# A hybrid decoder step on one core: block loads moved ahead of head loads, casts freed from ScalarE's copies, and an input split moved later

## The chip, the cores and the metric

The kernel runs on one core of a Trainium2 chip. The metric is the device time of one launch in microseconds. Five engines run side by side, each working through its own row of instructions in order: TensorE (PE, with its weight loads listed as PEld), VectorE (DVE), ScalarE (ACT), GpSimd (POOL) and SyncE, whose queue (SPq) issues most of the transfers. They meet by semaphores.

## What is computed

One layer of a decoder over 1024 prompt rows and 32 sample rows (8 sequences of 4), width 1024. The input is normalised and modulated, multiplied by a wide input matrix, and goes through two branches: an mLSTM with matrix memory (4 heads, chunks of 128) and sliding-window attention (8 query heads, 2 key heads, window 128, a sink per head). Each branch is gated and projected, the two are mixed by sigmoid gates, projected once more and added to the input.

```python
h, gate = adaln_in(x, c, w_ada, b_ada, g_norm)
(mq, mk, mv, mi, mf, mo, mz, aq, ak, av, az, gm, ga) = split_in(h @ w_in)
y_m, C, n, m = mlstm_branch(mq, mk, mv, mi, mf, mo, mz, C0, n0, m0, b_i, b_f, g_mn)
...
y_a = o.astype(x.dtype) * jax.nn.silu(az)
u = jax.nn.sigmoid(gm) * (y_m @ w_mo) + jax.nn.sigmoid(ga) * (y_a @ w_ao)
x = x + gate * (u @ w_o)
```

## The kernel before

All matmuls of the big projections are done in three products of rounded halves: each operand is split into a hi part (a cast to the rounded format, mostly on ACT) and a lo part (the remainder, a subtraction on DVE or GpSimd), and hi x hi, lo x hi and hi x lo are summed in PSUM. So every weight tile and every input tile passes through a cast and a subtraction before PE can use it. The names say which is which: `wh_...` and `wl_...` are the halves of a weight, `ym_l` and `ym_h` are the buffers of the halves of the gated mLSTM output (the names are those of the quarter of memory that they lie in: `ym_l` holds the hi part, `ym_h` the lo part).

The program runs in stages. First come the modulation and the first column groups. Then the queries of attention (`g_aq`) and the first head's `mq`, `mk`, `mv` and the second head's `mq` (`g_mq`) are computed column group by column group with plain products. From there the remaining input columns are computed in pairs as 2 x 2 blocks with seven products instead of eight (`block_products`, L1639). The stage that follows, the attention branch's output projection, uses the same scheme in four groups (`att_products`, L1851), and its products are written to PSUM tiles `ax`, `aw`, `az` and `ay`. Then the mLSTM output projection (`g_w_mo`) and the last projection (`fo...`) follow.

The code is written as one stream that emits PE's instructions in their final order. Beside it run generators (`Side`, L113): attention units, head steps, loads, sample work. Each generator yields an estimated time; when the emitted PE work has advanced that far it is resumed and emits its next piece. The rows of ACT and DVE are then put in order by a scheduler, which places an instruction early if its inputs look ready. What is emitted may be tied down with order-only links: `no_sync` (L215) puts one instruction of an engine behind another without a semaphore, and the wrapper `Ordered` (L225) links every ACT instruction that is emitted to those in `S.floor`, if there are any. `emptied` (L588) sets that floor to the copy just emitted:

```python
        def emptied(ins):
            if not products_done or begun_att:
                S.floor = [getattr(ins, "ins", ins)]
```

In the attention output stage it is called on every copy from one PSUM tile to another (`aw` from `ax`, `ay` from `aw`) and on the copy `p5` of `az`, and the floor stands until the next one.

Three places matter here.

The first block loads: `sum_blocks` (L1424) forms sums of input blocks for the seven products. Its second half waits until `plain_ends` is set (L1114, at the last plain job), polls every 0.5 us of planned time, loads two pairs of blocks `hb` from DRAM (four transfers of 256 KB), yields 3.0, and subtracts in each pair on DVE. The loads of the first head's first chunks (`hq`, `hk`, `hv`, `et`, `qw`; `load`, L1136) come from another generator at about the same place. All these tiles come from one rotating pool of 50 buffers (`ht`, L207), so the place in the row decides which old buffer a load has to wait for. Two attention units are under way there: `unit` (L894) computes scores `sc`, masks them on DVE with a row maximum (the custom operations into `p` and `mx`), exponentiates on ACT and transposes (`pt`) into PSUM; a copy brings `pt` back into `p`. The sample attention (`sample_attention`, L1003) ends with two transposes into `ost`. The tiles `pt`, `smp` and `ost` share the two PSUM buffers of the pool `pb` (L201).

The output stage's casts: `split` of `AttPair` (L1832) casts a weight block on ACT and subtracts on DVE for the seven products of one group; `split_ahead` in `att_products` calls it two products ahead. The names carry the group and the home: `ao0B` is group 0, home B, which serves product 6 and then product 2; `ao0C` serves 7 and 3, `ao0D` 4, `ao1A` the next group's 1 and 5. At the same time the last input gates (`hg`, L1612) and the sums of the attention output (`att_sums`, L1745, tiles `yr`, `yat...`, `yab...`) are still being finished on ACT, DVE and GpSimd.

The next stage's input: the mLSTM output `ymD` is loaded from DRAM and split into `ym_l` and `ym_h` (`split`, L1368), one quarter at product 6 of groups 0, 1 and 3 and one at product 3 of group 2.

Of the kernel before, what the change touches and what calls it, by code (L numbers as in the profile page):

```python
# [186 lines left out]
def body(tc, a):  # L187
    nc = tc.nc
    with ExitStack() as ctx:
# [17 lines left out]
        def ht(shape, name, dt=F32):  # L207
            return sp.tile(shape, dt, tag="half", bufs=50, name=name)
# [50 lines left out]
        V, S, G = Ordered(nc.vector, "V"), Ordered(nc.scalar, "S"), Ordered(nc.gpsimd, "G")  # L259
# [311 lines left out]
        def piece(w, rh, rl, kn, name, p, evac):  # L571
# [13 lines left out]
            evac(p, acc, c0, n)  # L585
            side.tick()

        def emptied(ins):  # L588
            if not products_done or begun_att:
                S.floor = [getattr(ins, "ins", ins)]  # L590

        def clear():
            while side.left <= 4:
                yield 0.0, ""

        hs, begun_att = {}, []

        def h_hi(k, c0, n, x="h"):
            ks = k
# [765 lines left out]
                store(a["n_s"], at["n1"])  # L1365


        def split(src, his, los, cols, k, eng=V):  # L1368
            for i, c in enumerate(cols):
                raw = ht([128, 512], "yr")[:, :c.stop - c.start]  # L1370
                dma(raw, src[k][:, c])
                hi, lo = his(k, c.start, c.stop - c.start), los(k, c.start, c.stop - c.start)
                S.copy(hi, raw)
                eng.tensor_tensor(lo, raw, hi.bitcast(F32), op=ALU.subtract)
# [49 lines left out]
        def sum_blocks():  # L1424
            names = "t3", "t2", "t4"
            for n in names:
                blocks[n] = []
            for k in range(4):
                b11, b12, b21, b22 = (xT[th][4 * kh + k] for kh in range(2) for th in range(2))
                for n in names:  # L1430
                    block_tiles(n, k)
                V.tensor_tensor(b22, b22, b12, op=ALU.subtract)
                yield 2.5, ""
                V.tensor_tensor(b11, b11, b22, op=ALU.add)
                V.tensor_tensor(b21, b21, b11, op=ALU.subtract)
                yield 4.0, ""
                for n, t in zip(names, (b22, b11, b21)):
                    block_split(n, k, t)
                    yield 3.0, ""
            formed.append("t2")  # L1440
            while not plain_ends:
                yield 0.5, ""
            load = lambda k: block_load(((0, 0), (0, 1)), k)
            ts = [load(0), load(1)]
            yield 3.0, ""
            for b11, b12 in ts:
                V.tensor_tensor(b12, b12, b11, op=ALU.subtract)
            while not products_done:
                yield 0.5, ""
            for k in range(4):  # L1450
                b11, b12 = ts[k]
                if k > 1:
                    V.tensor_tensor(b12, b12, b11, op=ALU.subtract)
                block_split("t1", k, b12)
                if k < 2:
                    ts.append(load(k + 2))
                yield 1.5, ""
            formed.append("t1")
# [180 lines left out]
        def block_products(jobs, hook):  # L1639
# [27 lines left out]
            for j, (n, i) in enumerate(flat):  # L1667
# [31 lines left out]
                if i == 6:  # L1699
                    Y = filled(pa, "by", W, n)  # L1700
                elif i == 2:
                    job_.done(0, 0, X)
                    gated_ = [job_.weighted] if job_.kind is query_gate else []
                elif i == 5:
                    p5 = ht([128, 512], "p5")
                    emptied(S.copy(p5, Z))
                elif i == 3:
                    job_.done(0, 1, p5, W)
                elif i == 4:
                    job_.done(1, 0, Y)  # L1710
# [140 lines left out]
        def att_products():  # L1851
# [23 lines left out]
            jobs[0].split(5)  # L1875
            yield
            ut.extend(quarter(x, [128, 4, PITCH], "u") for x in ("h1", "l1"))
            begun_att.append(True)
            for j, (n, i) in enumerate(flat):
                job_ = jobs[n]  # L1880
                nxt = jobs[n + 1] if n < 3 else None
                if i == 6:
                    if nxt:
                        nxt.landed = [last["PE"]]
                        nxt.gates()
                    if n in (0, 1, 3):
                        split(ymD, *ymx, PCOLS, {0: 2, 1: 3, 3: 1}[n], G if n == 3 else V)
                if i == 3 and n == 2:
                    split(ymD, *ymx, PCOLS, 0)
                if i == 2 and not nxt:  # L1890
                    for d in range(4):
                        preload(("w_mo", d))
                split_ahead(j + 2)
                if i == 3 and not nxt:
                    prefetch(("w_mo", 0))
                    gated(("w_mo", 0))
                if i == 1:
                    o = NX = pg([128, 512], "ax")
                elif i == 5:
                    o = Z = pa([128, 512], "az")  # L1900
                else:
                    o = {2: lambda: X, 3: lambda: W, 4: lambda: Y, 6: lambda: W, 7: lambda: Y}[i]()
                new = i in (1, 5)
                wh, wl = job_.w.pop(i)
                for k in range(2):
                    side.until(lambda: k in ya[OPERANDS[i]])
                    bh, bl = ya[OPERANDS[i]][k]
                    mm(o, wh[:, k], bh, start=(new and k == 0), stop=False, more=not new)
                    mm(o, wh[:, k], bl, start=False, stop=False, more=not new)
                    mm(o, wl[:, k], bh, start=False, stop=(k == 1), more=not new)  # L1910
                    side.tick()

                def copy_of(pool, name, src):
                    t = pool([128, 512], name)
                    if n == 0 and (j == 0 or i == 6):
                        mm(t, job_.g["A"][0][:, 0], ya["b11"][0][0], start=True, stop=True)
                    emptied(S.copy(t, src))
                    return t

                if i == 6:  # L1920
                    Y = copy_of(pa, "ay", W)
                    if not nxt:
                        job_.samples_end()
                elif i == 2:
                    job_.done(0, 0, X)
                    if nxt:
                        job_.samples_end()
                        side.now += nxt.cost
                        nxt.first_sums()
                elif i == 5:  # L1930
                    p5 = ht([128, 512], "p5")
                    emptied(S.copy(p5, Z))
                elif i == 7:
                    job_.done(1, 1, p5, Y)
                elif i == 3:
                    job_.done(0, 1, p5, W)
                elif i == 4:
                    job_.done(1, 0, Y)
                if j == 0 or (i == 3 and nxt):
                    X = NX  # L1940
                    W = copy_of(pg, "aw", X)
            S.floor = []


        def run(gen):
# [602 lines left out]
```

## Time and profile before

| what | value |
|---|---|
| time of three runs | 818.04, 820.47, 820.71 us, median 820.47 |
| the profiled execution's own time | 818.98 us |
| its span | 817.2 us |
| granted TensorE clock, mean | 0.996 |
| PE busy | 799.9 us, 98% of the span |
| DVE busy | 599.3 us, 73% |
| ACT busy | 419.0 us, 51% |
| POOL busy | 79.7 us, 10% |
| transfers | 165.51 MB, mean 203 GB/s |

The profile is of one execution. A row of a timeline gives the start in us from the span's start, the duration, the engine, the line, the operation and its tiles as out<-in, and in brackets how long the engine was idle before it and what ended that. Almost all computing instructions bear line 233 or 296, which are the helpers that record them; they are told apart by their tiles. PE matmuls overlap: the time that one costs is the distance from its start to the next start. A DMA instruction on SPq is only its issue; when the data lands is seen from who waits for it.

### The profile page before, as it was taken

The page shows a single profiled execution, that of the slowest core. Times are in us where ns is not written, and L with a number is a line of the kernel's source. Part 1 is how long each engine was busy: PE and PEld are TensorE (multiplying, and loading weights), DVE is VectorE, ACT ScalarE, POOL GpSimd, SP SyncE. Part 2 cuts the span into 40 slices and gives each one's busy share as a digit, 9 for nine tenths or more (in the row PEclk, how much of TensorE's full clock was granted, in tenths as well). Part 3 has the DMA queues.
Part 4 walks back from the last instruction along what each step waited for, and adds up shares of the span by engine and source line. Part 5 has one row for each costly group of instructions (what it writes and reads, how often), then busy time and mean ns, then how long its engine had stood idle before and what let it go on. Part 6 is the DMA issues. An engine that isn't in the chain of part 4 may idle for free. (4 is left out here: it accounts for less than half of the span.)

```text
span 817.2 us, 15181 instructions
## 1 busy us (share of the span) xinstructions
PE 799.9 (98%) x5162; PEld 669.0 (82%) x5162; DVE 599.3 (73%) x1502; ACT 419.0 (51%) x1021; POOL 79.7 (10%) x156
## 2 busy tenths in 40 slices
PE   8999999997999999999999999999999999999996
PEld 5779898896888888888888888888888779997775
DVE  5899986745756557476568888898668998875666
ACT  5664355654565564546656545554446553124335
POOL 0120000010000000000001323231002201000000
PEclk9999999999999999999999999999999999999999
DMA  9995667554744433547764685866246589748632
GB/s 351 375 340 159 209 191 194 180 174 143 213 154 142 140 102 134 155 150 239 253 217 132 248 255 193 285 208 195 101 135 209 171 279 347 262 150 294 207 104 110
DMA packets 113794, 165.51 MB, mean 203 GB/s; under 512 B 21248, under 2 KB 55936, under 8 KB 113684
## 3 DMA queue, kind: packets, MB, share of 16 engines
q1 hardware_dynamic: 107316, 152.21, 56.9%
q10 hardware_dynamic: 4752, 7.60, 2.5%
q0 software_dynamic: 1648, 4.72, 1.5%
q8 instruction: 41, 0.67, 0.3%
q14 instruction: 37, 0.30, 0.1%
HBM read 115.51 MB, written 50.00 MB: 203 GB/s over the span
## 5 line engine op out<-in xcount | busy, mean ns | idle before, releaser
L233 ACT ACTIVATE p<-p,nmx 128x256 f32<-128x256 f32 (+1 forms) x64 | 30.9, 484 | 17.6 <-DVE nmx L233 12.8
L233 DVE CUSTOM_DVE_ANT_0 p<-sc,cst,sink 128x256 f32<-128x256 f32 (+1 forms) x64 | 26.1, 463 | 13.2 <-PE sc L296 13.2
L233 POOL TENSOR_SCALAR Cs<-Cs,sxb 128x129 f32<-128x129 f32 x32 | 28.1, 896 | 42.4 <-PE sn L296 42.4
L296 PE MATMUL g_aq<-h_h,wh_aq 128*128 128x384 f32 (+1 forms) x96 | 32.2, 336 | 0.0
L296 PE MATMUL g_aq<-h_h,wl_aq 128*128 128x384 f32 (+1 forms) x96 | 30.9, 322 | 0.0
L296 PE MATMUL g_aq<-h_l,wh_aq 128*128 128x384 f32 (+1 forms) x96 | 30.8, 321 | 0.0
L296 PE MATMUL g_w_mo<-ym_l,wh_w_mo 128*128 128x384 f32 (+1 forms) x96 | 30.8, 321 | 0.0
L296 PE MATMUL g_w_mo<-ym_l,wl_w_mo 128*128 128x384 f32 (+1 forms) x96 | 30.8, 321 | 0.0
L296 PE MATMUL g_w_mo<-ym_h,wh_w_mo 128*128 128x384 f32 (+1 forms) x96 | 30.8, 321 | 0.0
L233 ACT CAST wosh<-wor 128x512 fp32r<-128x512 f32 x24 | 14.8, 621 | 14.0 <-DVE wor L233 13.2
L282 POOL DMA_DIRECT2D oD<-p x16 | 8.7, 544 | 132.5 <-ACT p L233 62.9
L233 DVE COPY p<-pt 128x512 f32<-128x512 f32 (+1 forms) x16 | 10.5, 657 | 14.8 <-PE pt L301 14.6
L296 PEld LDWEIGHTS g_aq<-h_h,wh_aq 128*128 128x128 f32 x96 | 18.0, 188 | 2.5 <-issue 1.5
L233 DVE TENSOR_TENSOR wosl<-wor,wosh 128x512 fp32r<-128x512 f32 x24 | 16.5, 686 | 3.3 <-ACT wosh L233 3.2
L233 DVE SCALAR_TENSOR_TENSOR tgw_mo<-tgw_mo,g_w_mo 128x384 f32<-128x384 f32 (+1 forms) x24 | 12.4, 518 | 8.1 <-PE g_w_mo L296 7.3
L296 PEld LDWEIGHTS g_w_mo<-ym_l,wl_w_mo 128*128 128x128 f32 x96 | 18.0, 188 | 0.1
L233 ACT ACTIVATE aq<-g_aq 128x384 f32<-128x384 f32 (+1 forms) x12 | 5.6, 463 | 24.4 <-PE g_aq L296 24.4
L296 PEld LDWEIGHTS g_w_mo<-ym_l,wh_w_mo 128*128 128x128 f32 x96 | 18.0, 188 | 0.0
L296 PEld LDWEIGHTS g_aq<-h_l,wh_aq 128*128 128x128 f32 x96 | 18.1, 188 | 0.0
L296 PEld LDWEIGHTS g_w_mo<-ym_h,wh_w_mo 128*128 128x128 f32 x96 | 18.0, 188 | 0.0
L296 PEld LDWEIGHTS g_aq<-h_h,wl_aq 128*128 128x128 f32 x96 | 18.0, 188 | 0.0
L233 DVE TENSOR_TENSOR et<-et,S 128x384 f32<-128x384 f32 (+1 forms) x12 | 6.1, 509 | 15.8 <-PE S L296 15.8
(2068 smaller groups left out, 2848.5 us busy)
## 6 DMA issues: line engine op xcount, KB each, us to landing
early_h<-w_ada SPq DMA_DIRECT2D x8, 512.0 KB, 10.1
adar_ga<-w_ada SPq DMA_DIRECT2D x16, 256.0 KB, 3.9
wr_ga<-w SPq DMA_DIRECT2D x16, 256.0 KB
wr_gm<-w SPq DMA_DIRECT2D x16, 256.0 KB, 6.8
taD<-gt SPq DMA_DIRECT2D x16, 256.0 KB, 2.3
tmD<-gt SPq DMA_DIRECT2D x16, 256.0 KB, 2.1
wor<-w_out SPq DMA_DIRECT2D x16, 256.0 KB, 7.3
tga<-taD SPq DMA_DIRECT2D x16, 256.0 KB, 3.5
```

The source lines that it names most:

```text
L233: ins = f(*args, **kw)
L282: ins = (eng or nc.sync).dma_start(out, in_)
L296: in_order(nc.tensor.matmul(out, lhsT, rhs, start=start, stop=stop, skip_group_check=more))
```

## The change

Three edits go together.

In `sum_blocks` the poll for `plain_ends` yields 0.0 instead of 0.5, so it is resumed at the next step of the planner, and the wait between loads and subtractions is 7.0 instead of 3.0 of planned time.

In `att_products` the floor is no longer set by `emptied` and no longer stands from copy to copy. The copies `aw` and `ay` are remembered in `emptied_last`, the copies `p5` are not, and the floor is set around `split_ahead` alone, from the third step on (j > 1), with the split of the next stage's input inside it.

The split of `ymD` is divided into its loads and its casts with subtractions. For groups 0 and 1 the loads stay at product 6, and the casts and subtractions move to product 4. For groups 2 and 3 nothing is divided.

```diff
         def emptied(ins):
-            if not products_done or begun_att:
-                S.floor = [getattr(ins, "ins", ins)]
+            if not products_done:
+                S.floor = [copy_made(ins)]
...
-        def split(src, his, los, cols, k, eng=V):
-            for i, c in enumerate(cols):
-                raw = ht([128, 512], "yr")[:, :c.stop - c.start]
+        def split_load(src, cols, k):
+            raws = [ht([128, 512], "yr")[:, :c.stop - c.start] for c in cols]
+            for raw, c in zip(raws, cols):
                 dma(raw, src[k][:, c])
+            return raws
+
+        def split(src, his, los, cols, k, eng=V, raws=None):
+            for c, raw in zip(cols, raws or split_load(src, cols, k)):
...
             while not plain_ends:
-                yield 0.5, ""
+                yield 0.0, ""
             load = lambda k: block_load(((0, 0), (0, 1)), k)
             ts = [load(0), load(1)]
-            yield 3.0, ""
+            yield 7.0, ""
...
-                    if n in (0, 1, 3):
-                        split(ymD, *ymx, PCOLS, {0: 2, 1: 3, 3: 1}[n], G if n == 3 else V)
+                    if n == 3:
+                        split(ymD, *ymx, PCOLS, 1, G)
+                    elif n < 2:
+                        ym_raws = split_load(ymD, PCOLS, n + 2)
...
+                if j > 1:
+                    S.floor = list(emptied_last)
                 split_ahead(j + 2)
+                if i == 4 and n < 2:
+                    split(ymD, *ymx, PCOLS, n + 2, V, ym_raws)
+                S.floor = []
...
-                    emptied(S.copy(t, src))
+                    emptied_last[:] = [copy_made(S.copy(t, src))]
...
                     p5 = ht([128, 512], "p5")
-                    emptied(S.copy(p5, Z))
+                    S.copy(p5, Z)
```

PE's row is the same in both kernels but for numbers in names. What moves is on SPq, DVE and ACT.

SPq's row at the end of the plain jobs, before; `hq` to `qw` are the first head's five loads, `hb_0` and `hb_1` the two pairs of blocks, the rows ahead and behind are a weight and the next attention unit's keys:

```order
L282 DMA wr_w_mo_0_2451<-w_mo 128x512
L282 DMA hq_0_2457<-qD_137 128x384
L282 DMA hk_0_2458<-kD_138 128x384
L282 DMA hv_0_2459<-vD_139 128x384
L282 DMA et<-nmd 128x384
L282 DMA qw<-wid 128x384
L282 DMA hb_0_2467<-hD 128x512
L282 DMA hb_0_2469<-hD 128x512
L282 DMA hb_1_2471<-hD 128x512
L282 DMA hb_1_2473<-hD 128x512
L282 DMA uqk<-kD 128x384
```

The same place of SPq's row now:

```order
L282 DMA wr_w_mo_0_2451<-w_mo 128x512
L282 DMA hb_0_2457<-hD 128x512
L282 DMA hb_0_2459<-hD 128x512
L282 DMA hb_1_2461<-hD 128x512
L282 DMA hb_1_2463<-hD 128x512
L282 DMA hq_0_2465<-qD_137 128x384
L282 DMA hk_0_2466<-kD_138 128x384
L282 DMA hv_0_2467<-vD_139 128x384
L282 DMA et<-nmd 128x384
L282 DMA qw<-wid 128x384
L282 DMA uqk<-kD 128x384
```

The four block loads stand ahead of the head's five, in the first four of the nine places, and nothing else has moved in this row in the whole program.

DVE's row at the same time, before; `ws` is a sum of weights, the ISA rows are the mask operations of one attention unit with their row maxima, and the COPY is that of another unit's transposed probabilities:

```order
L233 TENSOR_TENSOR ws_2591<-wr_mv_0_2447,wr_mv_1_2449 128x512
L233 TENSOR_TENSOR hb_0_2469<-hb_0_2469,hb_0_2467 128x512
L233 ISA p_2542,mx<-sc_4_0_2545,cst,sink 128x256
L233 ISA mx 128x1
L233 ISA p_2542,mx<-sc_4_0_2545,cst,sink 128x256
L233 ISA mx 128x1
L233 TENSOR_TENSOR hb_1_2473<-hb_1_2473,hb_1_2471 128x512
L233 ISA p_2543,mx<-sc_4_1_2546,cst,sink 128x256
L233 ISA mx 128x1
L233 ISA p_2543,mx<-sc_4_1_2546,cst,sink 128x256
L233 ISA mx 128x1
L233 COPY p_2301<-pt_0_1_2563 128x384
```

The same place of DVE's row now:

```order
L233 TENSOR_TENSOR ws_2589<-wr_mv_0_2447,wr_mv_1_2449 128x512
L233 TENSOR_TENSOR hb_0_2459<-hb_0_2459,hb_0_2457 128x512
L233 TENSOR_TENSOR hb_1_2463<-hb_1_2463,hb_1_2461 128x512
L233 ISA p_2540,mx<-sc_4_0_2543,cst,sink 128x256
L233 ISA mx 128x1
L233 ISA p_2540,mx<-sc_4_0_2543,cst,sink 128x256
L233 ISA mx 128x1
L233 ISA p_2541,mx<-sc_4_1_2544,cst,sink 128x256
L233 ISA mx 128x1
L233 ISA p_2541,mx<-sc_4_1_2544,cst,sink 128x256
L233 ISA mx 128x1
L233 COPY p_2301<-pt_0_1_2561 128x384
```

The second subtraction has moved ahead of the two mask operations that stood between the two; the copy is still behind both.

DVE's row in group 0 of the output stage, before; `hg` are the last input gates, `u_h` the gated results of the stage:

```order
L233 TENSOR_TENSOR yat2l_7779<-yr,yat2h_7778 128x512
L233 SCALAR_TENSOR_TENSOR hg_7688<-hg_7758,hg_7688 128x512
L233 TENSOR_TENSOR hg_7688<-hg_7688,ho 128x512
L233 SCALAR_TENSOR_TENSOR hg_7785<-hg_7785,by 128x512
L233 SCALAR_TENSOR_TENSOR hg_7785<-hg_7660,hg_7785 128x512
L233 TENSOR_TENSOR yr<-yr 128x512
L233 TENSOR_TENSOR hg_7785<-hg_7785,ho 128x512
L233 TENSOR_TENSOR wl_ao0B<-wr_ao_7592,wh_ao0B 128x256
...
L233 TENSOR_TENSOR yat4l_7855<-yr,yat4h_7854 128x512
L233 TENSOR_TENSOR ym_h_7557<-yr,ym_l_7556 128x384 x2
L233 TENSOR_TENSOR ym_h_7557<-yr,ym_l_7556 128x288
L233 SCALAR_TENSOR_TENSOR u_h_7790<-tga,u_h_7790 128x512
```

The same places of DVE's row now:

```order
L233 TENSOR_TENSOR yat2l_7779<-yr,yat2h_7778 128x512
L233 TENSOR_TENSOR wl_ao0B<-wr_ao_7592,wh_ao0B 128x256
L233 SCALAR_TENSOR_TENSOR hg_7688<-hg_7758,hg_7688 128x512
...
L233 TENSOR_TENSOR yat4l_7849<-yr,yat4h_7848 128x512
L233 SCALAR_TENSOR_TENSOR u_h_7790<-tga,u_h_7790 128x512
L233 TENSOR_TENSOR wl_ao0D<-wr_ao_7593,wh_ao0D 128x256
...
L233 TENSOR_TENSOR wl_ao1B<-wr_ao_7490,wh_ao1B 128x256
L233 TENSOR_TENSOR ym_h_7557<-yr,ym_l_7556 128x384 x2
L233 TENSOR_TENSOR ym_h_7557<-yr,ym_l_7556 128x288
L233 TENSOR_TENSOR wl_ao1B<-wr_ao_7490,wh_ao1B 128x256
```

The lo part for product 2 (`wl_ao0B`) has moved ahead of six instructions, and the three `ym_h` have moved from ahead of `wl_ao0D` to between the two `wl_ao1B` of the next group. On ACT the first cast into `wh_ao0B` has moved ahead of the cast of `yab22h`, and the second from behind the copy `aw` to the first one's old place.

More of the change, by code (lines that the diff above doesn't have):

```diff
@@ L586, in piece @@
             side.tick()
+        copy_made = lambda ins: getattr(ins, "ins", ins)
         def emptied(ins):
-            if not products_done or begun_att:
-                S.floor = [getattr(ins, "ins", ins)]
+            if not products_done:
+                S.floor = [copy_made(ins)]
         def clear():
@@ L594, in clear @@
                 yield 0.0, ""
-        hs, begun_att = {}, []
+        hs = {}
         def h_hi(k, c0, n, x="h"):
@@ L1877, in att_products @@
             ut.extend(quarter(x, [128, 4, PITCH], "u") for x in ("h1", "l1"))
-            begun_att.append(True)
+            emptied_last = []
             for j, (n, i) in enumerate(flat):
@@ L1931, in att_products @@
                     p5 = ht([128, 512], "p5")
-                    emptied(S.copy(p5, Z))
+                    S.copy(p5, Z)
                 elif i == 7:
@@ L1941, in att_products @@
                     W = copy_of(pg, "aw", X)
-            S.floor = []
         def run(gen):
```

## The prediction

> **What bounds the kernel now.** I read the page first, then the waits of TensorE (PE), then the timelines of PE, VectorE (DVE), ScalarE (ACT) and the load queue (SPq) around each of those waits, and last the chain of waits. The page's span and engine rows:
>
> ```profile
> span 817.2 us, 15181 instructions
> PE 799.9 (98%) x5162; PEld 669.0 (82%) x5162; DVE 599.3 (73%) x1502; ACT 419.0 (51%) x1021; POOL 79.7 (10%) x156
> ```
>
> PE is busy for 98% of the span, so all that a change of order can win is 817.2 - 799.9 = 17.3 us of idle PE, and whatever PE loses by running slowly. The waits of PE, longest first (total, times, longest), name three places of interest here:
>
> ```profile
> PE ost L301 <- DVE p L233: 4.1, 1, 4.1
> ...
> PE ay L296 <- DVE wl_ao0D L233: 0.9, 1, 0.9
> ...
> PE ax L296 <- DVE wl_ao0B L233: 0.8, 1, 0.8
> ```
>
> All three are waits for DVE. The first sits where the head loads and the first block loads are issued, the two others at the start of the output products of the attention branch: the two places that the change touches. After 652.61 us the chain of waits runs on PE alone to 787.7 us; its longest and its last piece before that:
>
> ```profile
> 681.78 45.96 PE g_w_mo L296 x288
> ...
> 784.96 2.73 PE foW L296 x12
> ```
>
> So what PE gains at either place arrives at the end, unless a later wait takes it back.
>
> **Part 1: the first blocks' loads.** PE's timeline (start, duration) around the first wait:
>
> ```profile
> 191.76 0.33 PE L296 MATMUL g_mq<-h_l,wh_mq 128*128 128x384 f32 x1
> 191.93 0.34 PE L296 MATMUL g_mq<-h_h,wl_mq 128*128 128x384 f32 x1
> 196.41 0.69 PE L301 MATMUL ost<-cst,ps 128*128 128x128 f32 x2 [4.14 <-DVE p L233]
> 196.75 0.67 PE L296 MATMUL g_mq<-h_h,wh_mq 128*128 128x384 f32 x1
> ...
> 199.78 0.36 PE L296 MATMUL g_mq<-h_h,wh_mq 128*128 128x384 f32 x1
> ```
>
> Matmuls of this shape start 0.17 us apart. The `ost` transposes would start at 191.93 + 0.17 = 192.10; they start at 196.41, so 4.3 us are lost. Then nine matmuls take 199.78 - 196.75 = 3.03 us where nine spacings are 9 x 0.17 = 1.53: another 1.5 us. The windows (busy us of PE, PEld, DVE, ACT and POOL, then the granted clock) show why:
>
> ```profile
> 196.00:198.00 2.00, 1.59 (x6) 1.59 (x7) 1.97 (x6) 1.49 (x6) 0.00 (x0) 0.60 0.52 199
> 198.00:200.00 2.00, 2.00 (x9) 2.00 (x8) 1.93 (x7) 1.19 (x5) 0.00 (x0) 0.55 0.00 0
> ```
>
> The granted clock is 0.60 and 0.55 right after the wait. The place costs 4.3 + 1.5 = 5.8 us. A rule for the second share: the Trainium skill, "TensorE: Matmul & The Clock Gate", section "Part 1: The HAM clock gate", has the clock halved after an idle window of about 3.4 us and restored after about 3.4 us of work, which as an estimate loses 1.7 us; by that page the place would cost 6.0 us. The trace agrees in kind (199.78 - 196.41 = 3.4 us at about half clock).
>
> Why PE waits: `ost` takes a PSUM buffer of the pool `pb`, of which there are two, and its last reader is DVE's copy of the transposed probabilities. DVE's timeline:
>
> ```profile
> 184.96 0.68 DVE L233 TENSOR_TENSOR ws<-wr_mv,wr_mv 128x512 f32<-128x512 f32 x1
> 191.01 0.69 DVE L233 TENSOR_TENSOR hb<-hb,hb 128x512 f32<-128x512 f32 x1 [5.37 <-DMA hb<-hD]
> 191.72 0.48 DVE L233 CUSTOM_DVE_ANT_0 p<-sc,cst,sink 128x256 f32<-128x256 f32 x1
> ...
> 194.38 0.69 DVE L233 TENSOR_TENSOR hb<-hb,hb 128x512 f32<-128x512 f32 x1 [1.77 <-DMA hb<-hD]
> ...
> 195.80 0.55 DVE L233 COPY p<-pt 128x384 f32<-128x384 f32 x1
> ```
>
> DVE is held twice, 5.37 and 1.77 us, by the two block subtractions, and the copy that PE needs is queued behind both. It ends at 196.35, and PE starts 0.06 us later. The loads, on SPq's timeline and in its waits between 176 and 187 us:
>
> ```profile
> 177.68 0.38 SPq L282 DMA_DIRECT2D hq<-qD  x1
> ...
> 184.65 0.32 SPq L282 DMA_DIRECT2D qw<-wid  x1
> 185.07 1.80 SPq L282 DMA_DIRECT2D hb<-hD  x4
> ```
>
> ```profile
> SPq L282 <- DMA vD<-mk: 13.6, 2, 8.5
> ```
>
> Four head loads go out from 177.68 on; the fifth, `qw`, is held until 184.65 by the landing of a `vD` store, and the four block loads stand behind it. The order shows the block loads in the first four places now, with the head's five behind them; the wait belongs to the place in the row (a buffer or a semaphore used before), so it will hold `hq`, the new fifth. The block loads then go out 7.4 us earlier (177.68 for 185.07). At worst they landed 194.38 - 185.07 = 9.3 us after the first was issued; from 177.68 that is 187.0. From there DVE needs at most one more subtraction (0.69), four mask operations (0.48 each, 1.9) and the copy (0.55): 187.0 + 3.2 = 190.2. PE asks at 192.1. The wait goes whole, with 1.9 us to spare, and the clock stays up: 5.8 us. Bounds: 6.0 above (the pair of transposes itself at full clock saves some 0.2 more), 5.1 below (a wait of 0.7 us, one DVE operation, for whatever is late next).
>
> What is late next is the head: its five loads now leave where the block loads left, from 184.65, and at the same worst landing arrive by 194.4. They are wanted here:
>
> ```profile
> 199.90 0.56 DVE L233 TENSOR_TENSOR et<-et,cst 128x384 f32<-128x384 f32 x1
> 203.57 0.49 PE L301 MATMUL tk<-cst,hk 128*128 128x128 f32 x3
> ```
>
> With everything 5.8 us earlier DVE asks for `et` at 194.1 and PE for `hk` at 197.8. DVE may wait 0.3 us, PE has 3.4 us to spare: nothing, as long as that cover stands; beyond it, 1 us per us.
>
> **Part 2: casts without a floor in the first two groups, and the split of the next stage's input later.** PE and then DVE:
>
> ```profile
> 644.06 0.39 PE L296 MATMUL ax<-yab21h,wh_ao0B 128*128 128x512 f32 x1
> 644.28 0.39 PE L296 MATMUL ax<-yab21l,wh_ao0B 128*128 128x512 f32 x1
> 645.48 0.50 PE L296 MATMUL ax<-yab21h,wl_ao0B 128*128 128x512 f32 x1 [0.81 <-DVE wl_ao0B L233]
> 645.82 0.39 PE L296 MATMUL ax<-yab21h,wh_ao0B 128*128 128x512 f32 x1
> ...
> 651.29 0.39 PE L296 MATMUL ay<-yat4l,wh_ao0D 128*128 128x512 f32 x1
> 652.61 0.50 PE L296 MATMUL ay<-yat4h,wl_ao0D 128*128 128x512 f32 x1 [0.93 <-DVE wl_ao0D L233]
> ```
>
> ```profile
> 645.02 0.41 DVE L233 TENSOR_TENSOR wl_ao0B<-wr_ao,wh_ao0B 128x256 fp32r<-128x256 f32 x1
> ...
> 650.23 1.38 DVE L233 TENSOR_TENSOR ym_h<-yr,ym_l 128x384 fp32r<-128x384 f32 x3
> 651.54 0.68 DVE L233 SCALAR_TENSOR_TENSOR u_h<-tga,u_h 128x512 f32<-128x512 f32 x1
> 652.14 0.41 DVE L233 TENSOR_TENSOR wl_ao0D<-wr_ao,wh_ao0D 128x256 fp32r<-128x256 f32 x1
> ```
>
> With a spacing of 0.23, the first wait costs 1.20 - 0.23 = 0.97 us and 0.11 for the slow restart (0.34 to the next start), the second 1.09 and as much again: 2.3 us, the ceiling. The first goes: `wl_ao0B` is now ahead of the six DVE instructions that stood between it and `yat2l`. For the second, DVE works without a pause up to `wl_ao0D`; its busy time is the third in this window's row:
>
> ```profile
> 639.40:652.50 13.10, 11.46 (x52) 8.82 (x50) 12.93 (x28) 7.24 (x17) 1.54 (x1) 1.00 0.63 194
> ```
>
> The set of instructions ahead of that one is the same as before but for the three `ym_h` subtractions, 651.54 - 650.23 = 1.3 us (the three loads keep their place in SPq's row). So `wl_ao0D` ends 1.3 us earlier and PE restarts at 651.3: PE comes to this wait 1.1 us earlier and finds most of it still there. The two waits together give 1.3, not 2.3.
>
> Against that stands a cast that now comes early in ACT's row: the hi part `wh_ao0B` before `yab22h`. It needs a weight buffer that PE still reads for its product 7:
>
> ```profile
> 631.72 0.39 PE L296 MATMUL by<-t3h,wl_phead_gate__7603 128*128 128x512 f32 x1
> 631.69 0.61 ACT L233 CAST yab22h<-yr 128x512 fp32r<-128x512 f32 x1
> ```
>
> The buffer is free at 632.11, the cast takes about 0.3 us, so `yab22h` starts at 632.4 or 632.5, 0.8 us late, and behind it the subtraction on GpSimd and the DVE instruction that waits for that. If nothing catches that up, 0.5 of the 1.3 is left. I take 1.2, because 20 us lie between that cast and `wl_ao0D`, and each wait of DVE for ACT or GpSimd in them takes up part of the delay; ends 0.5 and 2.3.
>
> Who pays for the later split: the same three `ym_h` now stand between the two `wl_ao1B`, which ended here:
>
> ```profile
> 654.73 0.75 DVE L233 TENSOR_TENSOR wl_ao1B<-wr_ao,wh_ao1B 128x256 fp32r<-128x256 f32 x2
> 656.86 0.39 PE L296 MATMUL ax<-yab21h,wl_ao1B 128*128 128x512 f32 x1
> ```
>
> Taken out ahead and put in again, they leave the end of the second `wl_ao1B` at 655.48, while PE asks 1.2 us earlier, at 655.66: 0.2 us of cover, and any miss costs its own length. The same move in the second group and the dropped floor behind the copy of `az` have no PE wait near them; I cost both at nothing.
>
> **Sum.** 5.8 + 1.2 = 7.0 us. The profiled execution took 818.98 us (span 817.2 and 1.8 around it): 812.0. It is 1.5 us below the median of the three timed runs, 820.47, from which the same sum gives 813.5. I forecast 813.0, between the two and nearer the median. A measurement of this kernel can tell about 0.3%, 2.5 us, from no change.
>
> **Rivals.**
> A wait that shrinks (10%): the block loads share their time with other transfers and land later than 187.0, by 4 us, say; then DVE's copy ends at 194.2 and PE still waits 2.1 us. Against it: the four places went out without a pause before. For the clock, the rows say that waits of 0.81 and 0.93 us are followed by a matmul of 0.50 and then by 0.39 again, so a wait of that size brings no slow clock; 4.14 does. The gain is 5.8 - 2.1 + 1.2 = 4.9, time 815.6.
>
> No gain in part 2 (16%): the early cast or the thin cover of 0.2 us eats the 1.2, or 0.5 more. Gain 5.3 to 5.8, time 814.7 to 815.2.
>
> Given back later (8%): PE's 7 us run into a load that does not move with PE in the last 160 us. Speaking against it, the chain of waits there is PE alone. Time 818 to 820.5.
>
> Slower (4%): the wait grows. All four mask operations and the copy now stand behind both subtractions, where two stood ahead of the second. If the second block landed only at 194.4, PE would start at 197.6, which is 1.2 later than now and eats part 2; from there on every us costs one. At a landing of 198 the time is 824.1. The point from which this decides is 16.7 us after the first issue, against 9.3 seen.
>
> **How the numbers follow.** The forecast has 62%, its own gain running from 5.1 + 0.5 to 6.0 + 2.3, that is 5.6 to 8.3 us: 809.7 (from the lowest run, 818.04) to 815.1 (from 820.71). With the first two rivals the range goes from 810.0 to 816.5. Faster by over 0.3%: 62 + 10 + 16 = 88%; within 0.3%: 8%; slower: 4%.
>
> **What will show it.** Right: no PE wait on `ost`; granted clock 1.00 in the windows that hold the nine `g_mq` matmuls; `hb` loads issued near 177.7 and DVE not idle ahead of the subtractions; `hq` held to about 184.7; `ax` without a wait on `wl_ao0B`, a wait of 0.6 to 1.0 us left on `wl_ao0D`; span near 810. Wrong: a PE wait on `ost`, `tk` or `tv` above 1 us, a PE wait on `wl_ao1B`, or `wl_ao0D` ending no earlier relative to PE's `ax`.

## The result and the profile after

The kernel after takes 811.95 us (median of 4 runs, 811.18 to 812.10) against 819.64 us of the kernel before (median of 4 runs beside it, 818.04 to 820.71): a ratio of 0.9906, 95% interval 0.9886 to 0.9926. The profiled execution took 812.10 us. From its page, the span and the engine row:

```profile
span 810.3 us, 15182 instructions
PE 798.5 (99%) x5162; PEld 668.2 (82%) x5162; DVE 598.8 (74%) x1502; ACT 418.5 (52%) x1021; POOL 78.9 (10%) x156
```

The span is 6.9 us shorter, PE's busy time 1.4 us: most of what went was idle PE, the rest is matmuls at the full clock. Where it went is read from four matmuls that PE runs in the same order in both kernels: the first `smp` (ahead of the first place), the first `tk` (behind it), the first `ax` and the first `g_w_mo` (ahead of and behind the groups of the output stage). PE's timeline of the kernel before (start, duration):

```profile
188.90 0.30 PE L296 MATMUL smp<-wr_mk,c 128*32 128x128 f32 x2 [0.24 <-ACT p L233]
...
203.57 0.49 PE L301 MATMUL tk<-cst,hk 128*128 128x128 f32 x3
...
639.50 0.39 PE L296 MATMUL ax<-ym_l,wh_ao0A 128*128 128x512 f32 x1
...
681.62 0.33 PE L296 MATMUL g_w_mo<-ym_l,wh_w_mo 128*128 128x384 f32 x1
```

and of the kernel after:

```profile
189.49 0.30 PE L296 MATMUL smp<-wr_mk,c 128*32 128x128 f32 x2 [0.24 <-ACT p L233]
...
198.25 0.49 PE L301 MATMUL tk<-cst,hk 128*128 128x128 f32 x3
...
634.19 0.39 PE L296 MATMUL ax<-ym_l,wh_ao0A 128*128 128x512 f32 x1
...
674.75 0.33 PE L296 MATMUL g_w_mo<-ym_l,wh_w_mo 128*128 128x384 f32 x1
```

| stretch of PE's row, us | before | after | difference |
|---|---|---|---|
| start to `smp` | 188.90 | 189.49 | +0.59 |
| `smp` to `tk` | 14.67 | 8.76 | -5.91 |
| `tk` to `ax` | 435.93 | 435.94 | 0.0 |
| `ax` to `g_w_mo` | 42.12 | 40.56 | -1.56 |
| `g_w_mo` to the end of the span | 135.58 | 135.55 | 0.0 |

Two stretches changed, at the two places of the change, and nothing was given back: from `tk` to `ax` PE took 435.9 us in both. The 0.59 us ahead of `smp` lies where the two programs are the same; a second profile of the kernel after had `smp` at 188.86. These two stretches are the measure in what follows, since they leave the scatter of the start out.

**The first place.** PE's row at `ost`, the windows (us of PE, PEld, DVE, ACT, POOL, then the granted clock) over the matmuls behind it, DVE, and the load queue, all of the kernel after:

```profile
192.52 0.34 PE L296 MATMUL g_mq<-h_h,wl_mq 128*128 128x384 f32 x1
192.69 0.38 PE L301 MATMUL ost<-cst,ps 128*128 128x128 f32 x2
192.83 0.42 PE L296 MATMUL g_mq<-h_h,wh_mq 128*128 128x384 f32 x1
```

```profile
192.00:194.00 2.00, 2.00 (x14) 1.97 (x14) 1.45 (x7) 1.75 (x7) 0.00 (x0) 1.00 0.93 235
194.00:196.00 2.00, 2.00 (x16) 1.97 (x15) 1.94 (x5) 0.80 (x2) 0.00 (x0) 1.00 0.56 159
```

```profile
185.54 0.69 DVE L233 TENSOR_TENSOR ws<-wr_mv,wr_mv 128x512 f32<-128x512 f32 x1
186.15 1.29 DVE L233 TENSOR_TENSOR hb<-hb,hb 128x512 f32<-128x512 f32 x2
188.57 0.48 DVE L233 CUSTOM_DVE_ANT_0 p<-sc,cst,sink 128x256 f32<-128x256 f32 x1 [1.14 <-issue]
...
190.19 0.55 DVE L233 COPY p<-pt 128x384 f32<-128x384 f32 x1
```

```profile
178.28 1.80 SPq L282 DMA_DIRECT2D hb<-hD  x4
186.49 0.32 SPq L282 DMA_DIRECT2D hq<-qD  x1
```

`ost` starts one spacing behind the matmul ahead of it. The two subtractions follow `ws` without a wait, the copy that frees `ost`'s PSUM buffer ends at 190.74, 1.95 us before PE asks, and the clock behind `ost` is 1.00 where it was 0.60 and 0.55. The hold of the queue is still there; it now stands ahead of `hq`.

**The second place.** PE's and DVE's rows:

```profile
641.71 0.40 PE L296 MATMUL ay<-yat3h,wl_ao0C 128*128 128x512 f32 x1
642.87 0.47 PE L296 MATMUL ax<-ym_l,wh_ao1A 128*128 128x512 f32 x1 [0.76 <-DVE u_h L233]
...
646.13 0.40 PE L296 MATMUL ay<-yat4h,wl_ao0D 128*128 128x512 f32 x1
```

```profile
635.28 0.42 DVE L233 TENSOR_TENSOR wl_ao0B<-wr_ao,wh_ao0B 128x256 fp32r<-128x256 f32 x1
...
638.43 0.69 DVE L233 TENSOR_TENSOR yr<-yr 128x512 f32<-128x512 f32 x1 [0.60 <-POOL yab21l L233]
...
642.04 0.68 DVE L233 SCALAR_TENSOR_TENSOR u_h<-tga,ax 128x512 f32<-128x512 f32 x1
...
645.51 0.42 DVE L233 TENSOR_TENSOR wl_ao0D<-wr_ao,wh_ao0D 128x256 fp32r<-128x256 f32 x1
```

PE no longer waits for `wl_ao0B` nor for `wl_ao0D`. A new wait stands between: the first `ax` of group 1 is written to the PSUM bank out of which DVE's `u_h` still reads the `ax` of group 0, and DVE comes to `u_h` only at 642.04, ends at 642.72, and PE starts at 642.87. It costs 642.87 - 641.71 - 0.23 = 0.93 us. On its way to `u_h` DVE itself stood 0.60 us for `yab21l`, a subtraction on GpSimd.

### The profile page after: what moved, and what is told of

Its sections match the earlier page's. It is cut to its first block, busy times and chain, and to the rows that moved or that the text cites. A ratio compares the mean times of both kernels' runs of the same rounds, so it can differ in the third digit from the quotient of the medians.

```text
span 810.3 us, 15182 instructions
## 1 busy us (share of the span) xinstructions
PE 798.5 (99%) x5162; PEld 668.2 (82%) x5162; DVE 598.8 (74%) x1502; ACT 418.5 (52%) x1021; POOL 78.9 (10%) x156
## 4 chain that ended last, share of the span: by engine, by line
PE 92%; DVE 3%; DMA 2%; ACT 1%; issue 1%; SPq 0%; ACTq 0%; DVEq 0%
PE by L296 12%; PE bx L296 12%; PE bw L296 12%; PE bz L296 6%; PE g_aq L296 6%; PE g_w_mo L296 6%; PE g_mq L296 3%; PE foW L296 3%; PE foY L296 2%; PE foX L296 2%; PE smp L296 2%; PE sc L296 2%; PE oT L296 2%; PE pt L301 2%; PE n L296 2%; PE g_mv L296 1%
```

## The experiments

The theory after the result: the first place gave 5.9 us because DVE's row stood on the block loads, and only because of that; the second gave 1.5 us because the row of DVE that PE's next operands and banks (the PSUM buffers that it writes to) come from got shorter by the three `ym_h`. The rivals are named with each run.

### Only the first part

```diff
-                yield 0.5, ""
+                yield 0.0, ""
             load = lambda k: block_load(((0, 0), (0, 1)), k)
             ts = [load(0), load(1)]
-            yield 3.0, ""
+            yield 7.0, ""
```

> The kernel before with only the block loads ahead of the first head's loads and the subtractions 7.0 behind them; the output's casts and splits as before. Theory: this part alone carries 5.9 us: from the first smp to the first tk PE takes 8.8 us (14.67 in before), ost does not wait, the clock stays 1.00 there, and the time is 813.6 to 814.2 (ratio 0.993). The waits of 0.8 us (ax on wl_ao0B) and 0.9 us (ay on wl_ao0D) stay. Rival one: the output's part brought the larger share, then 816 or more. Rival two: the two waits of the output stage come from where the stage falls in time, and go with this part alone, then 812.

Measured: 812.87 us, ratio 0.9924 (0.9908 to 0.9940); `smp` to `tk` 8.76, `ax` to `g_w_mo` 42.04, with the waits of 0.8 and 0.9 us. The part carries 5.9 us and leaves the output stage as it was; both rivals are out.

### Only the loads, only the lag

The two numbers of that edit alone: the first keeps 3.0, the second keeps 0.5.

> The kernel before with only the loads moved ahead; the first subtraction stays where it stood on DVE, in front of the masks. Theory: the landing is what the DVE row stood on, so moving the loads alone gives the same as both: smp to tk 8.8 us, 813.6 to 814.2. Rival: the place of the subtractions in DVE's row is what costs, and the loads land no earlier for the use made of them; then PE still waits 3 to 4 us at ost and the time is 818 to 820.

> The kernel before with only the lag from 3.0 to 7.0; the loads stay behind the first head's. In the program's order the first subtraction keeps its place in front of the masks and the second goes behind the copy of pt. Theory: the first subtraction still waits 5 us for its load, the second no longer stands in front of the copy: the copy ends at about 193.9 where PE asks at 192.1, so PE waits 1.5 to 2.2 us instead of 4.1, and smp to tk is 10.7 to 12.3 us, depending on whether a gap of 2 us lowers the clock: 815.7 to 817.2. Rival: the second number does all of it, 813.6 to 814.2; or nothing of it, 819.6.

Loads alone: 813.17 us, ratio 0.9927 (0.9911 to 0.9942), `smp` to `tk` 8.75: the same as both. The second number does nothing that the first hasn't done.

Lag alone: 815.22 us, ratio 0.9956 (0.9943 to 0.9968), `smp` to `tk` 10.27. DVE and then PE with the lag alone:

```profile
190.23 0.69 DVE L233 TENSOR_TENSOR hb<-hb,hb 128x512 f32<-128x512 f32 x1 [4.96 <-DMA hb<-hD]
...
192.56 0.55 DVE L233 COPY p<-pt 128x384 f32<-128x384 f32 x1
```

```profile
191.56 0.34 PE L296 MATMUL g_mq<-h_h,wl_mq 128*128 128x384 f32 x1
193.17 0.44 PE L301 MATMUL ost<-cst,ps 128*128 128x128 f32 x2 [1.27 <-DVE p L233]
```

The first subtraction still waits, 4.96 us, and the copy behind it ends at 193.11; the second subtraction no longer stands in between. PE waits 1.27 us instead of 4.14, a little less than expected, and the granted clock stays at 1.00. The profile is of the fastest of twelve executions, 814.17 us; the slowest took 819.19, so the wait can be longer in others. What PE loses at `ost` is set by when the last load that is waited for ahead of the copy lands.

### Late loads with nothing queued behind them

```diff
+            while "osm" not in hs:
+                yield 0.5, ""
+            with behind(V, hs["osm"]):
                 for b11, b12 in ts:
                     V.tensor_tensor(b12, b12, b11, op=ALU.subtract)
```

`hs["osm"]` holds the last copy out of `ost`; the loads stay behind the head's.

> The kernel before with the loads where they were and both subtractions held behind the copies of ost on DVE, so that nothing that PE needs there stands behind a load. Theory: the late landing costs nothing when no row stands on it: smp to tk 8.8 to 9.5 us, 813.6 to 814.5, as good as earlier loads. Rival: the sums are needed soon after (h_h and h_l of the blocks are split behind them), so that the lateness comes back as a wait of PE between 200 and 215; then 816 to 819.6.

Measured: 813.13 us, ratio 0.9926 (0.9912 to 0.9940), `smp` to `tk` 8.76. DVE:

```profile
188.03 0.48 DVE L233 CUSTOM_DVE_ANT_0 p<-sc,cst,sink 128x256 f32<-128x256 f32 x1 [2.34 <-issue]
...
189.66 0.56 DVE L233 COPY p<-pt 128x384 f32<-128x384 f32 x1
...
194.67 1.29 DVE L233 TENSOR_TENSOR hb<-hb,hb 128x512 f32<-128x512 f32 x2
```

The loads are as late as before, the subtractions run without a wait, and the gain is the same. So the lateness was harmless; standing on it in front of a copy that PE waits for was not. The rival, that the block sums themselves are wanted early, is out.

### The copy taken out of DVE's row

```diff
-                if kv:
+                if kv and (g, b0) != (2, 0):
                     V.tensor_copy(pT[kv][:, n0:], pt[:, n0:])
```

(else ScalarE copies; loads and subtractions as in before.)

> The kernel before, but the one copy of pt that ost's PSUM buffer waits for is made by ScalarE instead of DVE; loads, subtractions and all else as in before. Theory: the row on DVE still stands on the late loads until 195, and the next thing that PE needs from it is the copy of ost (its buffer is taken by the next pt): ost starts at 192 without a wait, and PE stands at pt instead, from 194.7 to about 198. The stall moves by one step: smp to tk 12.5 to 14.7 us, 817 to 819. Rival: this copy alone stood behind the loads in a way that matters, then smp to tk is 8.8 to 9.5 us and the time 813 to 814.

Measured: 819.92 us, ratio 1.0012 (0.9999 to 1.0026): no gain. `smp` to `tk` was 11.42, less than expected, since the second of the two stops lies behind the first `tk`. DVE, then PE:

```profile
193.46 0.69 DVE L233 TENSOR_TENSOR hb<-hb,hb 128x512 f32<-128x512 f32 x1 [7.30 <-DMA uqv<-qD]
...
200.28 0.46 DVE L233 COPY osm<-ost 64x64 f32<-64x64 f32 x2
```

```profile
200.84 0.52 PE L301 MATMUL tk<-cst,hk 128*128 128x128 f32 x3 [2.50 <-issue]
203.55 0.90 PE L301 MATMUL tv<-cst,hv 128*128 128x128 f32 x3 [2.19 <-ACT p L233]
```

`ost` ran at 192.62 without a wait, as expected. But the stall only moved: `tk` started right behind the end of the copy out of `ost` (200.74) and `tv` waited for ScalarE, whose own chain hangs on DVE's masks. I had expected it at `pt`; it was one user of the buffers further on. From `smp` to `ax` PE took 451.1 us, 450.6 in before and 444.7 in after. In this execution the first block's subtraction started 4.0 us after the first `smp`, against 2.1 in before (the profile names the landing of another load, `uqv`, as what ended its wait), so the 0.5 us more says nothing; that nothing was won does.

### How long a gap lowers the clock

The kernel with the lag alone, with the copy of `pt` made three times over:

```diff
                 if kv:
+                    for _ in range(3 if (g, b0) == (2, 0) else 1):
                         V.tensor_copy(pT[kv][:, n0:], pt[:, n0:])
```

> The kernel with only the subtractions' lag changed (loads late, second subtraction behind the copy, where PE stood 1.27 us at ost and the clock stayed 1.00), but the copy of pt is made three times over, so that PE stands there about 3 us; between 1.3 us (clock 1.00) and 4.1 us (clock 0.55 to 0.60 after it). Theory: a gap of 3 us costs 3 us and no clock: smp to tk 11.7 to 12.3 us, granted clock 1.00 in the 2 us behind it. Rival: the clock falls behind a gap of 3 us as behind one of 4: 13.2 to 13.8 us and 0.55 to 0.65 there.

Measured: 816.55 us, ratio 0.9970 (0.9959 to 0.9982), `smp` to `tk` 12.61. PE, and the windows behind:

```profile
192.06 0.34 PE L296 MATMUL g_mq<-h_h,wl_mq 128*128 128x384 f32 x1
194.42 0.44 PE L301 MATMUL ost<-cst,ps 128*128 128x128 f32 x2 [2.02 <-ACT smps L233]
...
195.59 0.52 PE L296 MATMUL g_mq<-h_h,wl_mq 128*128 128x384 f32 x1
...
199.18 0.38 PE L296 MATMUL g_mq<-h_h,wh_mq 128*128 128x288 f32 x1
```

```profile
194.00:196.00 2.00, 1.58 (x9) 1.58 (x10) 2.00 (x5) 1.95 (x10) 0.00 (x0) 0.89 0.34 73
196.00:198.00 2.00, 2.00 (x8) 1.91 (x7) 1.93 (x7) 0.62 (x1) 0.00 (x0) 0.50 0.54 201
198.00:200.00 2.00, 2.00 (x15) 2.00 (x14) 1.97 (x5) 1.54 (x4) 0.00 (x0) 0.76 0.26 98
```

The gap was 2.0 us and not 3, so the edit did not do what it was made for: PE waited here for ScalarE's copy into `smps`, which stood behind an activation that waits for DVE's masks, and not for the third copy of `pt`, which began only at 194.59, behind the start of `ost`. With the lag alone `ost` had started ahead of that copy into `smps`. So `ost` seems to have taken the other of the two PSUM buffers here; the profile does not show which. The clock fell all the same. My theory, that a gap of 3 us costs only itself, is wrong, since even one of 2 us did not, and the rival holds in kind; its numbers were for a gap of 3 us and were not reached. Of the 12.61 - 8.76 = 3.85 us, 194.42 - 192.06 - 0.17 = 2.19 are idle, and 1.66 are left for the slow matmuls from 195.59 to 199.18.

### The second part and its halves

Only the second part (the first part's two numbers as in before); then the kernel after with the later split taken back (`split(ymD, ...)` at product 6 again); then the kernel after with the floor as in before and the later split kept.

> The kernel after with the block loads and their lag as in before: only the output stage is changed. Theory: the two parts do not touch each other; from the first ax of the output stage to the first g_w_mo PE takes 40.5 to 40.7 us (42.12 in before, 40.56 in after), the stall at ost stays (smp to tk 13.5 to 15 us), and the time is 1.5 us under before: 817 to 818. Rival: part of the output stage's gain hangs on the earlier part (loads that land earlier relative to it), then 41.5 to 42.1 there and no gain.

> The kernel after, but the next stage's input is split at product 6 again, cast and subtraction right behind their loads; the casts freed from the copies stay. Theory: DVE's row is full, so the time is set by where in it the rows that PE needs stand: the wait on wl_ao0B goes, ax waits 0.8 us on u_h as in after, and the three subtractions ym_h (about 1.5 us) stand in front of wl_ao0D again, which PE then waits 0.9 to 1.3 us for. First ax to first g_w_mo 41.4 to 41.9 us against 42.05 with the loads' part alone; 812.6 to 813.0. Rival: each edit ends one wait of its own and nothing else, then 40.9 here and about 812.2.

> The kernel after, but the output's casts stand behind ScalarE's copies from the first group on, as in before; the split at product 4 stays. Theory: the wait on wl_ao0B (0.8 us) stays, and because PE is that much later, u_h and wl_ao0D are both there when it asks: no other wait. First ax to first g_w_mo 40.6 to 41.0 us; 811.9 to 812.4: the later split brings nearly all of the second part's gain, the freed casts almost nothing. Rival: each edit ends one wait of its own, then 40.9 here as for the other half and both halves add up to the whole; it is told apart by the other half, which it puts at 40.9 too.

The whole second part alone: 817.56 us, ratio 0.9982 (0.9971 to 0.9993), `ax` to `g_w_mo` 40.57, `ost` waiting 4.1 us. The parts are independent.

Freed casts without the later split: 813.31 us, ratio 0.9933 (0.9919 to 0.9947), 42.10: nothing over the first part alone (42.04). Later split without freed casts: 811.81 us, ratio 0.9913 (0.9898 to 0.9928), 40.55: all of it. Both rivals, each edit ending a wait of its own, are out: they put both at 40.9. The theory for the freed casts, 41.4 to 41.9, left them a small gain, and there was none. The waits of PE in the output stage, freed casts first, later split second:

```profile
PE ay L296 <- DVE wl_ao0D L233: 1.0, 1, 1.0
PE ax L296 <- DVE u_h L233: 0.7, 1, 0.7
```

```profile
PE ax L296 <- DVE wl_ao0B L233: 0.8, 1, 0.8
```

Freeing the casts ended the wait for `wl_ao0B` and opened the one for `u_h`. Why is seen when the rows are counted from the first `ax` (start, us; the last line belongs to the next run):

| kernel | DVE `u_h` | PE `ax` of group 1 | DVE `wl_ao0D` | PE on `wl_ao0D` | `g_w_mo` |
|---|---|---|---|---|---|
| before | 7.86 | 8.84 | 12.64 | 13.11 | 42.12 |
| freed casts | 7.85 | 8.68 | 12.63 | 13.10 | 42.10 |
| later split | 7.88 | 8.87 | 11.35 | 12.06 | 40.55 |
| after | 7.85 | 8.68 | 11.32 | 11.94 | 40.56 |
| after, `u_h` first | 6.39 | 7.79 | 10.60 | 11.38 | 40.13 |

`u_h` stands at 7.85 to 7.88 in the first four, wherever `wl_ao0B` stood ahead of it. DVE has the same instructions up to there in all four, but it does not spend the time alike, and GpSimd's subtraction `yab21l` has a hand in it. GpSimd and DVE in before, then GpSimd in after:

```profile
641.80 1.54 POOL L233 TENSOR_TENSOR yab21l<-yr,yab21h 128x512 fp32r<-128x512 f32 x1 [4.03 <-ACT yab21h L233]
```

```profile
642.81 1.07 DVE L233 SCALAR_TENSOR_TENSOR hg<-hg,hg 128x512 f32<-128x512 f32 x1
```

```profile
636.49 1.91 POOL L233 TENSOR_TENSOR yab21l<-yr,yab21h 128x512 fp32r<-128x512 f32 x1 [4.02 <-ACT yab21h L233]
```

In before, and with the later split alone, one `hg` takes 1.07 us beside `yab21l` and there are some short pauses. With the freed casts, and in after, that `hg` comes later and takes 0.68 us, but GpSimd takes 1.9 us instead of 1.54 and DVE stands 0.6 us for it. Counted at 0.60 us from the start of one 128x512 instruction to the next, the first costs DVE 0.82 us and the second, with another short pause, 0.80, so that `u_h` stands at the same place is in part chance; whether it would come earlier with a shorter `yab21l` was not tried. PE reaches the first `ax` of group 1 within 0.2 us of the same place in all four, having waited at `wl_ao0B` or at `u_h`. What moves the later rows is what leaves the row ahead of them: the three `ym_h`, 1.3 us, between `u_h` and `wl_ao0D`.

### `u_h` ahead of the next weights

```diff
-                split_ahead(j + 2)
+                early = (n, i) == (0, 2)
+                if j == 6:
+                    V.floor = []
+                if not early:
+                    split_ahead(j + 2)
...
                     job_.done(0, 0, X)
+                    if early:
+                        V.floor = [V.before]
+                        split_ahead(j + 2)
```

> The kernel after, but for group 0 DVE's u_h out of ax is put ahead of the next weight's sums and subtractions (wr_ao, wl_ao1A, ws), which are held behind it. Theory: the 0.8 us that ax still waits in after is for the PSUM bank that u_h reads, and u_h could run 1.5 us earlier; the wait goes, and the rows put behind it have more than 1 us to spare: first ax to first g_w_mo 39.6 to 39.9 us (40.56 in after), 810.9 to 811.3. Rival: the row is full, so whatever is put behind is waited for instead (wl_ao1A, wh_ao1A or wl_ao0D by PE), 40.3 to 40.8 us and 811.7 to 812.2.

Measured: 811.65 us, ratio 0.9911 (0.9896 to 0.9926); `ax` to `g_w_mo` 40.13. `u_h` moved 1.46 us ahead and the wait for it went, but 0.43 us came of it and not 0.7 to 1.0: PE now stops for 0.3 us at `wl_ao0C` and for 0.1 and 0.2 at `wl_ao1B`, rows that stand behind. Between the theory and its rival, then. The time of the whole can't be told from that of the kernel after.

### One subtraction given to GpSimd

```diff
-        ASIDE = [(n, k) for n in ("b22", "b21", "t3") for k in range(2)]
+        ASIDE = [(n, k) for n in ("b22", "b21", "t3") for k in range(2)] + [("t4", 1)]
```

on top of `u_h` first, beside the kernel after on the same chip.

> The kernel with u_h ahead of the next weight's rows (40.13 us from the first ax to the first g_w_mo, with 0.1 to 0.3 us gaps left at wl_ao0C and wl_ao1B), and DVE's subtraction yat4l given to GpSimd, which is idle there. Theory: DVE's row is what is left, and 0.6 us less in it ends the gap at wl_ao0C: 39.6 to 39.9 us, about 0.3 us less than with yat4l on DVE. Rival: GpSimd's subtraction of 1.5 to 1.9 us slows the DVE rows beside it (one small DVE operation took 1.28 us instead of 0.18 us beside yat3l), 40.1 to 41 us.

> The kernel after, unchanged, on the same chip as the run with u_h first and yat4l on GpSimd, to compare the two. Both theories: first ax to first g_w_mo 40.56 us, smp to tk 8.76 us, time 811.5 to 812.2.

Measured: 811.73 us, ratio 0.9915 (0.9898 to 0.9932), and 811.42 us, ratio 0.9914 (0.9899 to 0.9929), for the kernel after. `ax` to `g_w_mo` 40.34, more than the 40.13 without GpSimd and less than the 40.54 of after. GpSimd and DVE:

```profile
641.04 1.29 POOL L233 TENSOR_TENSOR yat4l<-yr,yat4h 128x512 fp32r<-128x512 f32 x1 [2.37 <-ACT yat4h L233]
```

```profile
640.86 0.68 DVE L233 SCALAR_TENSOR_TENSOR u_h<-tga,ax 128x512 f32<-128x512 f32 x1
641.46 1.16 DVE L233 TENSOR_TENSOR wl_ao1A<-wr_ao,wh_ao1A 128x256 fp32r<-128x256 f32 x1
```

`wl_ao1A` took 1.16 us beside GpSimd's subtraction where it takes 0.42 without: 0.74 lost for 0.6 saved. The rival holds. The Trainium skill, "SBUF — State Buffer", section "Who interferes with whom", says that a VectorE instruction with two SBUF inputs contends with a GpSimd instruction that reads SBUF, and calls the port pair that the two share an exclusive lock. The trace agrees: `wl_ao1A` ends at 642.62, 0.29 us behind the end of `yat4l`. No version tried here beats the kernel after by more than can be measured.

## Why the prediction was right, and which steps of it failed

**The sum** was 5.8 + 1.2 = 7.0 us; the two stretches gave 5.91 + 1.56 = 7.47. The time forecast, 813.0, is 1.05 us over the 811.95 measured. The lower end of its range was put at 810.0 where its own working gives 809.7; nothing hangs on it.

**The first part** went as argued in its cause and its size: the block loads left the queue at 178.28 (177.7 forecast, and this execution ran 0.6 us late there), the hold stayed with the place in the queue, PE had 1.95 us to spare (1.9), and the clock stayed up. That the copy ended at 190.74, where the sum had 190.2 at the latest (190.8 in the time of this late execution), is luck: the sum ran from the landing of the loads, but both subtractions were done at 187.44 and the first mask began only at 188.57. It began at the same place, 0.92 us ahead of the first `smp`, in the run where the subtractions stand behind the masks, so it did not wait for the loads; PE's scores `sc`, which the masks read, end 0.13 us ahead of it. The cause, DVE's row standing on a landing, is shown from both sides: earlier loads alone give all of it, and late loads with the subtractions behind the copies give all of it too. Mis-sized was the head: it left the queue at 186.49, not 184.7, and `qw` at 189.82, yet DVE came to `et` at 195.19 without a wait.

**The second part** was right in its sum and wrong in what it made of the two edits. "The first goes: `wl_ao0B` is now ahead of the six DVE instructions" held as a row of the trace, but it brought nothing. The prediction's own reason for the rest, that only the three `ym_h` leave DVE's row, is what the runs bear out: 1.3 us expected from them, 1.5 measured with the later split alone. That DVE works without a pause up to `wl_ao0D` held before and not after, where it stood 0.60 us for GpSimd. The wait that was to be left, 0.6 to 1.0 us on `wl_ao0D`, came with 0.76 us two products earlier, on `u_h`. The step that failed is the list of what PE needs from DVE: I had followed the operands of the matmuls and not the banks they write to. The other 0.2 to 0.3 us lie in the later groups: before loses nearly 0.2 us each in PE's row at `wl_ao2B` and `wl_ao3B`, which it still does with the freed casts alone and no longer with the later split alone.

**The early cast** of `wh_ao0B` did delay `yab22h`, by 0.5 us (the 0.8 was an upper end): it starts at 626.93 where before's 631.69 less the 5.31 us that PE is early makes 626.38. DVE's next `yr` came to its old place all the same (634.63 before, 629.33 after), so nothing was paid.

**The thin cover** at the second `wl_ao1B` was 0.2 us by the forecast and about nothing in the trace: it ends at 650.17, PE's matmul starts at 650.24.

**The rivals.** The wait did not shrink to a rest, it went; but that rival was priced too low: I took a gap of 2.1 us to leave the clock alone, and one of 2.0 us lowered it for 1.66 us. Its time would have been nearer 817 than 815.6. The slower case, a landing that eats the spare, decided from a landing 16.7 us after the first issue; here the two subtractions ran without a wait from 186.15 on, 7.9 us after it.

## What to carry to other kernels

Where an engine waits for another's copy, look at what that copy is queued behind: an instruction that waits for a load, put ahead in an in-order row, hands its lateness to all that stands behind it, and either an earlier load or a later instruction ends that. Where such a row is nearly full, moving work inside it mostly moves the wait to the next row that is needed; count what leaves the row ahead of the last row needed, list both the operands and the buffers that the waiting engine needs from it, and look whom the row itself waits for. Moving the one row that was named in the waits, the copy or the cast, won nothing in either place here.

## What the runs showed of the hardware

Gaps of 0.76 and 1.27 us in PE's work left the granted clock at 1.00; gaps of 2.02 and 4.14 us were followed by 3.4 to 3.6 us at about half clock, which cost 1.66 and 1.5 us: about the same for these two, each seen in one profiled execution. Two gaps of 2.50 and 2.19 us close together, in the run with the copy on ScalarE, lowered it as well (0.77 and 0.50 in the windows from 202 to 206). Behind the 2.02 us gap PE ran 1.1 us at full clock first (194.42 to about 195.5). The Trainium skill, "TensorE: Matmul & The Clock Gate", section "Part 1: The HAM clock gate", has the clock fall after an idle window of about 3.4 us and rise after a busy one of about 3.4 us, and the window free-running. The trace agrees with the length of the slow stretch; it does not agree with the idle time needed, for which 2.02 us were enough here.

The kernels in which PE waits behind a load scatter more. Their times spread over 2.4 to 5.1 us: 60 runs of before lay between 816.28 and 821.38 us, 12 of the lag alone between 814.17 and 819.19. Without such a wait they spread over 1.0 to 2.3 us: 5 with the subtractions behind the copies lay between 812.71 and 813.73, 6 with the loads alone between 812.40 and 814.66, 10 of the kernel after between 810.97 and 812.19. The counts differ, and that it is the landing that scatters was not measured by itself; in the profiles of before and of the lag alone the first block's subtraction started 2.1 and 1.7 us after the first `smp`, with the copy on ScalarE 4.0 us.
